# Attention on one core: the maxima's transposition, the one-over-sums products and VectorE's order rearranged

## The chip, the cores and the metric

The kernel runs on one core of one Trainium2 chip. The metric is the device time of one execution in microseconds; of several executions the median counts. A profiled execution has a time of its own and a span (first to last instruction), on which the trace is laid out.

## The reference, cut to what matters

One layer of a bidirectional encoder: attention, a residual layer norm, then a mixture of 32 experts (top 4 of 32, 1024 tokens) and another layer norm. The change touches attention alone. With 1024 tokens, 16 query heads in 4 groups of 4, and 64 values per head, the reference computes

```
q = rope(rms_norm(q)); k = rope(rms_norm(k))
for each block of 128 queries:
    s = einsum('bqkgd,bskd->bkgqs', q_blk, k) * HEAD_DIM ** -0.5
    p = softmax(s, axis=-1)
    o = einsum('bkgqs,bskd->bqkgd', p, v)
return o @ w_o
```

## The kernel before, in words

Attention runs as 32 groups: group n is a block of 128 queries (i = n // 4) with one group of four heads (g = n % 4). I call the groups of a block g0 to g3. Every group has eight steps k, one for each 128 keys. The loop over n and k near the end of the attention part writes out TensorE's order by hand (`manual_schedule` for PE); the orders of the other engines come from a planner, which may bring an instruction forward or put it off.

A step of group n issues on TensorE:

- `probs(n, k)`: two products into a PSUM tile `st` (128 keys by 512 queries; two such tiles in turn). The first is keys times queries, the second carries a correction and subtracts the maxima, which stand in rows 64 to 67 of the operand `q2s[n % 3]`. ScalarE then takes the exponential (`pt`), and GpSimd adds the eight `pt` of a group up in `acc`.
- `scores(n + 2, k // 2, k % 2)`: half of the scores of one head, two groups ahead, into a PSUM tile `sc` (two banks; two such tiles in turn). After the second half (odd k) VectorE takes the negated maximum over 1024 keys (line 434, tile `nm`). So each group has four of these maxima, m = 0 to 3, at k = 1, 3, 5 and 7.

Once in a group come:

- `maxima_a(n + 1)`: a transposition of the four maxima on TensorE (`tpm`, line 147) and on VectorE a product that spreads them over the rows of `q2s` (line 148). Its PSUM tile is one of tag `tp`, of which there is one buffer.
- `maxima_b(n + 1)`: ScalarE copies the queries into the other rows of `q2s`.
- `stack_q` (in g1 and g2): four transpositions (`tpq`, line 163) of the next block's queries, also into tag `tp`, which ScalarE (lines 165, 166) and VectorE (lines 167, 168) read.
- `pv(n - 1)`: 32 products of probabilities and values into the PSUM tile `po` (one buffer), and `close_a`, ScalarE's copy out of it.
- `late_sum(n - 1)`: VectorE adds the last `pt` to `acc` (line 452).

Once in a block of four groups come `scale_a` (in g0, behind `pv`: products `su` that sum over the keys, into tag `tp`, then on VectorE the reciprocal and three more instructions, lines 479 to 484) and `scale_b` (twice: a product `rb` into tag `tp` that spreads the reciprocals, and VectorE's product with the output, line 492).

Products and transpositions through the helper `mm` all show line 55. Each of the PSUM tags `tp` and `po` has one buffer, so a new tile of such a tag waits for all readers of the last one.

Of the kernel before, what the change touches and what calls it, by code (L numbers as in the profile page):

```python
# [9 lines left out]
F32 = mybir.dt.float32  # L10
# [10 lines left out]
P = 128  # L21
T = 1024
D = 1024
NT = T // P
# [3 lines left out]
HD = 64  # L28
# [17 lines left out]
def trunk_kernel(ctx: ExitStack, tc: tile.TileContext, x, w_qkv, q_norm, k_norm, w_o,  # L46
                 lnm_g, lnm_b, lnf_g, lnf_b, r_w, r_b, w_gu, b_gu, w_dn, b_dn,
                 rope_c, rope_s, out):
    nc = tc.nc
# [4 lines left out]
    def mm(o, lhsT, rhs, start=True, stop=True):  # L54
        nc.tensor.matmul(o, lhsT=lhsT, rhs=rhs, start=start, stop=stop)  # L55
# [49 lines left out]
    vn = p_kv.tile([P, NT, NKV, HD], F32, name="vn")  # L105
# [26 lines left out]
    def first_scores(s, ps):  # L132

        hf, m = divmod(s, 4)
        if s == 0:
            nms[0] = p_xq.tile([P, 4], F32R, tag="nm", bufs=3, name="nm0")
            nms["h"] = p_xq.tile([P, 4, 2], F32, name="nmh")
        sc = ps.tile([P, 512], F32, tag="qkv2", name=f"sc0_{s}")
        mm(sc, qs[0][:, m, :], kT_hi[:, 0, hf * 512:(hf + 1) * 512])
        nc.vector.tensor_reduce(nms["h"][:, m, hf:hf + 1], sc, AX.X, ALU.max, negate=True)  # L140
        if s == 7:
            nc.vector.tensor_reduce(nms[0], nms.pop("h"), AX.X, ALU.min)

    def maxima_a(n, ps):

        tp = ps.tile([P, 4, P], F32, tag="tp", name=f"tpm{n}")
        nc.tensor.transpose(tp[0:4, 0, :], nms.pop(n).bitcast(F32), ident)
        nc.vector.tensor_tensor(q2s[n % 3][HD:HD + 4], tp[0:4, 0:1, :].to_broadcast([4, 4, P]),  # L148
                                ident[0:4, 0:4, None].to_broadcast([4, 4, P]), ALU.mult)

    def maxima_b(n):
        i, g = divmod(n, NKV)
        nc.scalar.copy(q2s[n % 3][0:HD], qs[i][0:HD, 4 * g:4 * g + 4, :].bitcast(F32))
# [20 lines left out]
    with tc.tile_pool(name="p1", bufs=1, side="right", reuse_waits="tile") as p1, \  # L174
# [18 lines left out]
        def turn_x(i):  # L193
            xt = xts[i]
            xT = p_xq.tile([P, 2 * KD, P], F32R, tag="cols", bufs=2, name=f"xT{i}")
            hi, lo = xT[:, 0:KD, :], xT[:, KD:, :]
            for h in range(2):
                tp = ps1.tile([P, 4, P], F32, tag="tp", name=f"tp{i}_{h}")
                for c in range(4):
                    k = 4 * h + c  # L200
                    nc.tensor.transpose(tp[:, c, :], xt[:, k * P:(k + 1) * P], ident)
                split(hi[:, 4 * h:4 * h + 4, :], lo[:, 4 * h:4 * h + 4, :], tp)
            xTs[i] = (hi, lo)
            if i + 1 < NT:
                load_x(i + 1)
            else:
                load_q(0)

        def proj(i, k, j):
            hi, lo = xTs[i]  # L210
            sl = slice(j * 512, (j + 1) * 512)
            mm3(qkvs[i][j], hi[:, k, :], lo[:, k, :], wh[k][:, sl], wl[k][:, sl], k == 0, k == KD - 1)

        def open_qkv(i):
            t = {j: ps1.tile([P, 512], F32, tag=f"qkv{j}", name=f"qkv{i}_{j}") for j in (0, 2, 1)}
            qkvs[i] = [t[j] for j in range(3)]
# [4 lines left out]
        pe_order = ExitStack()  # L221
# [99 lines left out]
        for i in range(NT):  # L321
            k0 = (KD, late)[i] if i < 2 else 0
            if i > 1:
                open_qkv(i)
            for k in range(k0, KD):
                proj(i, k, 2)
            if 1 < i < NT - 1:
                turn_x(i + 1)
            norm_k(i)
            if i == NT - 1:  # L330
                stack_q(0, 0, ps1)
                stack_q(0, 1, ps1)
            for k in range(k0, KD):
                proj(i, k, 0)
                if i == NT - 1 and k % 2 == 1:
                    first_scores(k // 2, ps1)
            take_q(i, 0)
            if i == 0:
                take_q(i, 1)
            turn_k(i)  # L340
            if i == 0:
                turn_x(2)
            norm_q(i, 0)
            for k in range(k0, KD):
                proj(i, k, 1)
                if i == NT - 1 and 0 < k < 5:
                    first_scores(k + 3, ps1)
                if i == NT - 1 and k == 6:
                    maxima_a(0, ps1)
                    maxima_b(0)  # L350
            if i > 0:
                take_q(i, 1)
            norm_q(i, 1)
            if i == 1:
                in_order.close()
# [61 lines left out]
    with tc.tile_pool(name="p2", bufs=1, side="right", reuse_waits="tile") as p2, \  # L417
# [4 lines left out]
        pts, po, ot, sc, accs, rrs = [{} for _ in range(6)]  # L422
        NG = NT * NKV
# [27 lines left out]
        def late_sum(n):  # L451
            nc.vector.tensor_tensor(accs[n], accs[n], pts[n, NT - 1], ALU.add)

        def pv(n):

            i, g = divmod(n, NKV)
            po[n] = ps_o.tile([P, 2, P], F32, tag="po", name=f"po{n}")
            for k in range(NT):
                for a in range(2):
                    mm(po[n][a * HD:(a + 1) * HD].rearrange("p j t -> p (j t)"), vn[:, k, g, :],  # L460
                       pts[n, k][:, 2 * a * P:(2 * a + 2) * P], k == 0, k == NT - 1)
            for k in range(NT):
                del pts[n, k]

        def close_a(n):
            i, g = divmod(n, NKV)
            if g == 0:
                ot[i] = p2.tile([P, KD, P], F32, tag="ot", bufs=2, name=f"ot{i}")
            nc.scalar.copy(ot[i][:, 2 * g:2 * g + 2, :], po.pop(n))

        def scale_a(i):

            su = ps_t.tile([P, 4, P], F32, tag="tp", name=f"su{i}")
            for m in range(4):
                for g in range(NKV):
                    mm(su[g * NE:(g + 1) * NE, 0, :], which[:, m].rearrange("p r m -> p (r m)"),
                       accs[NKV * i + g][:, m * P:(m + 1) * P], m == 0, m == 3)
            rs = p2.tile([P, P], F32, tag="rs", bufs=1, name=f"rs{i}")
            nc.vector.reciprocal(rs, su[:, 0, :])
            hi = p2.tile([P, P], F32R, tag="rh", bufs=1, name=f"rh{i}")  # L480
            nc.vector.tensor_copy(hi, rs)
            nc.vector.scalar_tensor_tensor(rs, hi.bitcast(F32), low, rs, ALU.mult, ALU.subtract)
            rrs[i] = p2.tile([P, KD, P], F32R, tag="rr", bufs=1, name=f"rr{i}")
            nc.vector.tensor_tensor(rrs[i], rs[:, None, :].to_broadcast([P, KD, P]),
                                    col.rearrange("p g j -> p (g j)")[:, :, None].to_broadcast([P, KD, P]), ALU.mult)
# [39 lines left out]


        pe_order = ExitStack()
        pe_order.enter_context(tc.manual_schedule(engines={mybir.EngineType.PE}))
        for n in range(NG + 1):
            i, g = divmod(n, NKV)  # L530
            for k in range(NT):
                if k == (6 if n == 0 else 2) and n + 1 < NG:
                    maxima_a(n + 1, ps_t)
                if n < NG:
                    probs(n, k)
                if n == 0:
                    for m in range(2):
                        scores(1 + k // 4, k % 4, m)
                elif n + 2 < NG:
                    scores(n + 2, k // 2, k % 2)  # L540
                if n < NG and i + 1 < NT and g == 0 and k == 6:
                    load_q(i + 1)
                if k == (7 if n == 0 else 3) and n + 1 < NG:
                    maxima_b(n + 1)
                if k == 3 and n > 0:
                    if g in (1, 2) and i + 1 < NT:
                        stack_q(i + 1, g - 1, ps_t)
                    if n < NG - 1:
                        late_sum(n - 1)
                    pv(n - 1)  # L550
                    close_a(n - 1)
                    if g == 0:
                        scale_a(i - 1)
                if i > 0:
                    if (g, k) == (1, 5) or n == NG and k == 5:
                        scale_b(i - 1, 0)
                    if (g, k) == (1, 7) or n == NG and k == 7:
                        scale_b(i - 1, 1)
            if i in (2, 3) and g == 2:
                load_o(i - 2)  # L560
            if i == 4 and g == 2:
                load_xr(0)
# [790 lines left out]
    for i in range(NT // 2):  # L1353
        f = slot(order[(len(seq) + 1 + i) % len(order)], f"fs{i}")
# [13 lines left out]
    with tc.tile_pool(name="gen", bufs=1, side="right", reuse_waits="tile") as gp, \  # L1368
# [5 lines left out]
        with tc.For_i(0, n_blk, 1) as b:  # L1374
# [33 lines left out]
            for n in range(4):  # L1408
                w = gp.tile([P, KD, 512], F32, tag="gw", bufs=2, name=f"gwg{n}")
                nc.sync.dma_start(w, w_gu[ds(ev, 1), :, n * 512:(n + 1) * 512].rearrange("o (k p) n -> p (o k) n", p=P))  # L1410
                ps = gps.tile([P, 512], F32, tag="gu", bufs=2, name=f"ggu{n}")
# [6 lines left out]
            for n in range(2):  # L1418
                w = gp.tile([P, KD, 512], F32, tag="gw", bufs=2, name=f"gwd{n}")
                nc.sync.dma_start(w, w_dn[ds(ev, 1), :, n * 512:(n + 1) * 512].rearrange("o (k p) n -> p (o k) n", p=P))  # L1420
                ps = gps.tile([P, 512], F32, tag="gu", bufs=2, name=f"gy{n}")
# [87 lines left out]
```

## Time and profile before

| what | value |
|---|---|
| median of three runs | 2080.12 us (2079.3 to 2083.51) |
| the profiled execution's own time | 2075.34 us |
| its span | 2073.5 us |
| TensorE busy, of the span | 97% |
| VectorE, ScalarE, GpSimd busy, of the span | 77%, 62%, 26% |
| the 32 groups of attention | from 162 to about 520 us of the span |

TensorE's busy time counts the pipelined length of a product, which is longer than the spacing at which products follow one another. Where one engine's order is written by hand, its stalls are best read from the start times of neighbouring instructions: a step that has nothing to wait for shows the shortest spacing, and what goes beyond it is a wait or a switch.

### The profile page before, as it was taken

Reading aid. Unit: us, or ns where it says so; the run is one execution under the profiler, and the core shown is the slowest. Engines: PE = TensorE matmul, PEld = TensorE weight load, DVE = VectorE, ACT = ScalarE, POOL = GpSimd, SP = SyncE. Lnnn points to the kernel's source line nnn. Section 1 sums busy time; section 2 is a strip of 40 time slices with the busy share of each in tenths; the row PEclk is TensorE's granted clock in tenths of the full one; section 3 lists DMA queues with packets and bytes.
Section 4 is the critical chain, followed back from the end, with each engine's and each line's share of the span. In section 5 each row is a group of like instructions: output and inputs, shape, how many; then the busy total and the mean of one; then the engine's idle time right before and its main releaser. Section 6 shows DMA issues by size and latency. Waiting matters only on the chain. (4 is left out here: it accounts for less than half of the span.)

```text
span 2073.5 us, 28716 instructions
## 1 busy us (share of the span) xinstructions
PE 2011.8 (97%) x10691; PEld 1419.5 (68%) x10691; DVE 1601.8 (77%) x1649; ACT 1282.0 (62%) x1566; POOL 538.2 (26%) x373
## 2 busy tenths in 40 slices
PE   8998999999997999999999999999999999999997
PEld 6775666665675666666666767767777677677774
DVE  6647777776887877767777878878878788887894
ACT  5655655654554656566666766667667676676774
POOL 1216777775144211111102111101021121010100
PEclk9999999999998999999999999999999999999999
DMA  5216000000645777888788898978989889789875
GB/s 174 72 62 178 31 32 21 32 21 21 228 149 211 276 287 271 298 294 291 285 315 312 347 338 304 377 289 342 338 319 354 310 315 367 284 346 337 329 314 183
DMA packets 106352, 500.44 MB, mean 241 GB/s; under 512 B 16001, under 2 KB 17026, under 8 KB 73442
## 3 DMA queue, kind: packets, MB, share of 16 engines
q1 hardware_dynamic: 87360, 447.02, 56.0%
q0 software_dynamic: 16000, 50.90, 9.0%
q8 instruction: 85, 1.39, 0.3%
q10 hardware_dynamic: 2850, 0.66, 0.2%
q14 instruction: 57, 0.47, 0.1%
HBM read 457.05 MB, written 41.49 MB: 240 GB/s over the span
## 5 line engine op out<-in xcount | busy, mean ns | idle before, releaser
L55 PE MATMUL gu<-wh,xTh 128*128 128x512 f32 x1024 | 415.3, 406 | 1.0 <-ACT xTh L63 1.0
L55 PE MATMUL gu<-wh,xTl 128*128 128x512 f32 x1024 | 410.1, 400 | 0.0
L55 PE MATMUL gu<-wl,xTh 128*128 128x512 f32 x1024 | 401.9, 393 | 0.0
L1299 POOL DMA_INDIRECT fd<-y,mi x32 | 79.1, 2472 | 655.4 <-ACT y L1298 655.4
L448 POOL TENSOR_TENSOR acc<-acc,pt 128x512 f32<-128x512 f32 x152 | 211.8, 1394 | 78.3 <-ACT pt L444 68.7
L55 PEld LDWEIGHTS gu<-wh,xTh 128*128 128x128 f32 x1024 | 193.3, 189 | 42.4 <-ACT xTh L63 1.7
L55 PEld LDWEIGHTS gu<-wl,xTh 128*128 128x128 f32 x1024 | 193.3, 189 | 39.6 <-issue 0.2
L55 PEld LDWEIGHTS gu<-wh,xTl 128*128 128x128 f32 x1024 | 193.7, 189 | 38.8 <-issue 3.6
L55 PE MATMUL yp<-wl,aTh 128*128 128x512 f32 x512 | 204.2, 399 | 0.4 <-DVE wl L612 0.4
L55 PE MATMUL yp<-wh,aTh 128*128 128x512 f32 x512 | 201.6, 394 | 0.0
L55 PE MATMUL yp<-wh,aTl 128*128 128x512 f32 x512 | 199.7, 390 | 0.0
L434 DVE TENSOR_REDUCE nm<-sc 128x1 fp32r<-128x1024 f32 x124 | 150.6, 1221 | 50.5 <-PE sc L55 49.5
L444 ACT ACTIVATE pt<-st 128x512 f32<-128x512 f32 x256 | 149.4, 596 | 55.9 <-PE st L55 46.3
L598 POOL DMA_INDIRECT xg<-xd,mi x32 | 53.4, 1670 | 298.5 <-PE tpx L1136 288.9
L55 PE MATMUL qkv<-wh,xT 128*128 128x512 f32 x384 | 123.9, 403 | 2.6 <-ACT xT L63 1.4
L55 PEld LDWEIGHTS yp<-wh,aTh 128*128 128x128 f32 x512 | 96.2, 188 | 33.6 <-ACT act L1180 14.3
L55 PE MATMUL po<-pt,vn 128*64 128x256 f32 x1024 | 117.6, 382 | 0.0
L55 PE MATMUL st<-qs,kT_hi 128*128 128x512 f32 x256 | 112.5, 440 | 2.9 <-ACT pt L444 2.2
L55 PEld LDWEIGHTS yp<-wl,aTh 128*128 128x128 f32 x512 | 96.3, 188 | 21.9 <-DVE wl L612 1.2
L55 PEld LDWEIGHTS yp<-wh,aTl 128*128 128x128 f32 x512 | 96.1, 188 | 19.5
L55 PE MATMUL st<-q,kT_lo 128*128 128x512 f32 x256 | 102.2, 399 | 1.3 <-DVE q L148 1.3
L55 PE MATMUL sc<-kT_hi,qs 128*128 128x512 f32 x256 | 101.9, 404 | 1.0 <-DVE nm L434 0.8
(520 smaller groups left out, 4159.0 us busy)
## 6 DMA issues: line engine op xcount, KB each, us to landing
w0g<-in_expert_w_gate_up SPq DMA_DIRECT2D x8, 1024.0 KB, 7.1
w1g<-in_expert_w_gate_up SPq DMA_DIRECT2D x8, 1024.0 KB, 7.6
w2g<-in_expert_w_gate_up SPq DMA_DIRECT2D x8, 1024.0 KB, 9.6
w3g<-in_expert_w_gate_up SPq DMA_DIRECT2D x8, 1024.0 KB, 8.6
w4g<-in_expert_w_gate_up SPq DMA_DIRECT2D x8, 1024.0 KB, 6.9
w5g<-in_expert_w_gate_up SPq DMA_DIRECT2D x8, 1024.0 KB, 7.4
w6g<-in_expert_w_gate_up SPq DMA_DIRECT2D x8, 1024.0 KB, 6.5
w7g<-in_expert_w_gate_up SPq DMA_DIRECT2D x8, 1024.0 KB, 7.1
```

Of the source, the lines that this page charges most:

```text
L55: nc.tensor.matmul(o, lhsT=lhsT, rhs=rhs, start=start, stop=stop)
L434: nc.vector.tensor_reduce(nms[n][:, m:m + 1], sc.pop((n, m)), AX.X, ALU.max, negate=True)
L444: nc.scalar.activation(pts[n, k], st, AF.Exp)
L448: (nc.vector if n == NG - 1 or n == NG - 2 and k > 3 else nc.gpsimd).tensor_tensor(accs[n], pts[n, 0] if k == 1 else accs[n], pts[n, k], A ...
L598: return nc.gpsimd.indirect_dma_start(out=xg[e], out_offset=None, in_=xd, in_offset=bass.IndirectOffsetOnAxis(ap=mi[:, e:e + 1] if rows is ...
L1299: nc.gpsimd.indirect_dma_start(out=fd, out_offset=bass.IndirectOffsetOnAxis(ap=mi[:, e:e + 1], axis=0), in_=y, in_offset=None, bounds_chec ...
```

## The change

`maxima_a` takes its PSUM tile from its caller. For groups 2 to 31 the four maxima are transposed at step 3 instead of ahead of step 2, into columns 256 to 383 of the `po` tile, which is now a whole bank (512 columns), with the values' products behind it in columns 0 to 255. The call of `maxima_b` follows that of `stack_q`. `late_sum` keeps its place in g0 and moves to step 4, behind `pv`, in the other groups; the last `pt` of a group lives until then. The two `scale_b` move from g1 (steps 5 and 7) to g3 (steps 1 and 5). VectorE's order is written out too: inside the loop it follows the order of the code.

```
-    def maxima_a(n, ps):
+    def maxima_a(n, tp):
-        tp = ps.tile([P, 4, P], F32, tag="tp", name=f"tpm{n}")
         nc.tensor.transpose(tp[0:4, 0, :], nms.pop(n).bitcast(F32), ident)
...
-                    maxima_a(0, ps1)
+                    maxima_a(0, ps1.tile([P, 4, P], F32, tag="tp", name="tpm0"))
...
         def pv(n):
-            po[n] = ps_o.tile([P, 2, P], F32, tag="po", name=f"po{n}")
             for k in range(NT):
                 for a in range(2):
-                    mm(po[n][a * HD:(a + 1) * HD].rearrange("p j t -> p (j t)"), vn[:, k, g, :],
+                    mm(po[n][a * HD:(a + 1) * HD, 0:2, :].rearrange("p j t -> p (j t)"), vn[:, k, g, :],
                        pts[n, k][:, 2 * a * P:(2 * a + 2) * P], k == 0, k == NT - 1)
-            for k in range(NT):
+            for k in range(NT - 1):
                 del pts[n, k]
...
-            nc.scalar.copy(ot[i][:, 2 * g:2 * g + 2, :], po.pop(n))
+            nc.scalar.copy(ot[i][:, 2 * g:2 * g + 2, :], po.pop(n)[:, 0:2, :])
...
-        pe_order.enter_context(tc.manual_schedule(engines={mybir.EngineType.PE}))
+        pe_order.enter_context(tc.manual_schedule(engines={mybir.EngineType.PE, mybir.EngineType.DVE}))
         for n in range(NG + 1):
             i, g = divmod(n, NKV)
             for k in range(NT):
-                if k == (6 if n == 0 else 2) and n + 1 < NG:
-                    maxima_a(n + 1, ps_t)
+                if n == 0 and k == 6:
+                    maxima_a(n + 1, ps_t.tile([P, 4, P], F32, tag="tp", name="tpm1"))
                 if n < NG:
                     probs(n, k)
...
-                if k == (7 if n == 0 else 3) and n + 1 < NG:
+                if n == 0 and k == 7:
                     maxima_b(n + 1)
                 if k == 3 and n > 0:
+                    po[n - 1] = ps_o.tile([P, 4, P], F32, tag="po", name=f"po{n - 1}")
+                    if n + 1 < NG:
+                        maxima_a(n + 1, po[n - 1][:, 2:3, :])
                     if g in (1, 2) and i + 1 < NT:
                         stack_q(i + 1, g - 1, ps_t)
-                    if n < NG - 1:
+                    if n + 1 < NG:
+                        maxima_b(n + 1)
+                    if g == 0 and n < NG - 1:
                         late_sum(n - 1)
                     pv(n - 1)
                     close_a(n - 1)
                     if g == 0:
                         scale_a(i - 1)
+                if k == 4 and g > 0 and 0 < n < NG - 1:
+                    late_sum(n - 1)
                 if i > 0:
-                    if (g, k) == (1, 5) or n == NG and k == 5:
+                    if (g, k) == (3, 1) or n == NG and k == 5:
                         scale_b(i - 1, 0)
-                    if (g, k) == (1, 7) or n == NG and k == 7:
+                    if (g, k) == (3, 5) or n == NG and k == 7:
                         scale_b(i - 1, 1)
```

## Rows read from the trace of the kernel before

**Rows 1.** Windows view: two stretches, busy times of each engine, granted clock, DMA.

```profile
187.40:200.90 13.50, 10.62 (x63) 6.83 (x62) 8.62 (x8) 7.35 (x14) 7.99 (x7) 1.00 1.04 232
...
342.93:386.92 43.99, 42.23 (x271) 27.53 (x271) 34.05 (x34) 25.77 (x46) 33.03 (x25) 1.00 0.07 25
```

**Rows 2.** Waits view, 162 to 520 us: total us, times, longest.

```profile
PE tpq L163 <- DVE q L148: 7.4, 14, 2.8
...
PE tpm L147 <- DVE nm L434: 3.9, 7, 0.6
```

**Rows 3.** Timeline, TensorE, end of a g2 and start of the g3 behind it.

```profile
376.67 0.40 PE L55 MATMUL sc<-kT_hi,qs 128*128 128x512 f32 x1
376.91 0.47 PE L55 MATMUL st<-qs,kT_hi 128*128 128x512 f32 x1
...
378.16 0.40 PE L55 MATMUL sc<-kT_hi,qs 128*128 128x512 f32 x1
...
378.72 0.50 PE L55 MATMUL st<-qs,kT_hi 128*128 128x512 f32 x1
...
379.99 0.40 PE L55 MATMUL sc<-kT_hi,qs 128*128 128x512 f32 x1
380.32 3.67 PE L55 MATMUL po<-pt,vn 128*64 128x256 f32 x32
```

**Rows 4.** Timeline, TensorE, the g1 and g2 ahead of it.

```profile
354.35 0.40 PE L55 MATMUL sc<-kT_hi,qs 128*128 128x512 f32 x1
...
355.06 0.40 PE L55 MATMUL sc<-kT_hi,qs 128*128 128x512 f32 x1
...
356.10 0.48 PE L55 MATMUL st<-qs,kT_hi 128*128 128x512 f32 x1
...
357.35 0.40 PE L55 MATMUL sc<-kT_hi,qs 128*128 128x512 f32 x1
357.92 0.66 PE L163 MATMUL tpq<-ident,ql 128*128 128x128 f32 x4 [0.17 <-DVE q L148]
358.50 3.67 PE L55 MATMUL po<-pt,vn 128*64 128x256 f32 x32
...
365.01 0.40 PE L55 MATMUL sc<-kT_hi,qs 128*128 128x512 f32 x1
...
366.14 0.40 PE L55 MATMUL st<-qs,kT_hi 128*128 128x512 f32 x1
...
368.81 0.40 PE L55 MATMUL sc<-kT_hi,qs 128*128 128x512 f32 x1
...
370.31 3.67 PE L55 MATMUL po<-pt,vn 128*64 128x256 f32 x32
```

**Rows 5.** Timeline, VectorE, the same block.

```profile
350.96 0.96 DVE L479 RECIPROCAL rs<-su 128x128 f32<-128x128 f32 x1 [0.53 <-PE su L55]
...
354.80 2.35 DVE L434 TENSOR_REDUCE nm<-sc 128x1 fp32r<-128x1024 f32 x2
357.18 0.68 DVE L148 TENSOR_TENSOR q<-tpm,ident 4x512 fp32r<-4x512 f32 x1
...
365.06 0.69 DVE L492 TENSOR_TENSOR ot<-ot,rb 128x512 f32<-128x512 f32 x1
...
377.11 1.22 DVE L434 TENSOR_REDUCE nm<-sc 128x1 fp32r<-128x1024 f32 x1 [0.27 <-PE sc L55]
```

**Rows 6.** Timeline, VectorE, the last `scale_a`, with nothing between its instructions.

```profile
519.91 0.96 DVE L479 RECIPROCAL rs<-su 128x128 f32<-128x128 f32 x1 [2.88 <-PE su L55]
...
521.55 1.22 DVE L484 TENSOR_TENSOR rr<-rs,col 128x1024 fp32r<-128x1024 f32 x1
```

**Rows 7.** Timeline, ScalarE and VectorE, the readers of `tpq` in group 2.

```profile
194.36 0.58 ACT L165 CAST qs<-tpq 64x512 fp32r<-64x512 f32 x1 [3.11 <-PE tpq L163]
194.96 0.58 ACT L166 CAST odd<-tpq 64x512 fp32r<-64x512 f32 x1
...
195.57 0.68 DVE L167 TENSOR_TENSOR qs<-tpq,qs 64x512 fp32r<-64x512 f32 x1 [0.71 <-ACT odd L166]
```

## Prediction

> **What bounds the kernel now.** I read the windows view first, cut at the first product of each group, to see what a steady block of four groups costs: 43.99 us, with TensorE busy for 42.23 of them and the clock granted in full [rows 1]. VectorE has 34 us of work in it and ScalarE 26, so TensorE is the bound, and what counts is what makes TensorE wait or switch. The waits view of the attention stage comes next. TensorE's waits there are few: 7.4 us for line 148 ahead of the transpositions of `stack_q`, 3.9 us of the maxima's transposition for the last maximum [rows 2]. They are what this change can win. The TensorE timeline then gives prices by neighbouring starts. The reader is to see three spacings in it. A product follows `sc` after 0.24 us when nothing intervenes; with the maxima's transposition between, the spacing is 0.56 us, so it costs 0.32 [rows 3]. In g1 the same place takes 1.04 us, so 0.80 more than normal, since the transposition there waits for a maximum [rows 4]. And from the `sc` of step 3 to the first product of `pv` it takes 0.33 us in g3 (and, as the steps repeat, in g0), 1.15 in g1 and 1.50 in g2, where `stack_q` and its wait lie between [rows 3, 4].
>
> **What the move to the values' bank does.** The transposition itself moves to where TensorE changes over to `pv` anyway, and its 0.32 us (0.80 in g1, next to nothing in g2) leave step 1. But VectorE's line 148 now reads the bank into which `pv` writes next, and `pv` stands behind it in the code. The question is whether `pv` has to wait for that read although the columns differ. The trace has a case of its own: line 167 reads partitions 0 to 63 of a `tpq` tile and needs, as data, only line 165. Line 165 ended at 194.94, VectorE was idle, and yet line 167 began at 195.57, 0.03 us after the end of line 166, which reads partitions 64 to 127 of the same tile [rows 7]. So in this program accesses by two engines to one PSUM bank wait for each other, even reads of different halves. I take it that `pv` waits for line 148.
>
> The Trainium skill, "PSUM — Partial Sum Buffer", section "PSUM bank collisions raise a hardware error", states that two engines must not be at one bank in the same 32 partitions at one time, whichever addresses they touch. Line 148 reads partitions 0 to 3 and `pv` begins in partitions 0 to 63, so by that rule the wait is needed and the sum is the one below; a guard by address would give rival A's time. The trace is stricter than the rule, which lets different quadrants of a bank go together, as lines 166 and 167 would be.
>
> **The price of that wait.** In the code order that VectorE now follows, the maximum m = 1 of step 3 stands ahead of line 148, since `scores` is called before `maxima_a`. From the start of the last `sc` product: 0.44 us until VectorE begins the maximum (376.67 to 377.11) [rows 3, 5], 1.23 for it, 0.03 to the next instruction (354.80 + 2.35 to 357.18), 0.68 for line 148 [rows 5], 0.06 until TensorE goes on (357.86 to 357.92) [rows 4, 5]. `pv` starts 2.44 us behind `sc`, where it started after 0.33, 1.15 or 1.50. The step so gains 2.11 us in g0 and g3, 1.29 in g1, 0.94 in g2. The transpositions of `stack_q` (0.58 us, [rows 4]) no longer wait for line 148, and lie inside the wait. The transposition's own wait for the maxima ends too: they are ready over a step earlier. Nothing else hides these 2.44 us: the exponentials ahead are done and those behind need `st` products that stand behind `pv`.
>
> **The one-over-sums products.** In g1 they cost two spacings and a wait: step 5 one product (0.24), step 7 from `sc` to `st` 1.13 instead of 0.24, so 0.89 [rows 4], together 1.13. In g3 I charge one spacing each, 0.48. There is a side effect in g3: VectorE's product for the first of them (0.69, [rows 5]) now stands ahead of the step-3 maximum. It ends 0.44 + 1.23 + 0.03 + 0.69 = 2.39 us after the `sc` of step 1 and VectorE is ready 0.03 later; the `sc` of step 3 comes 1.83 - 0.32 = 1.51 behind that of step 1 [rows 3], plus the `rb` product 0.24, and is complete 0.44 later, at 2.19. The maximum, and so `pv`, are 0.23 late. The store of the block's output on SP's queue comes half a block later; it is read a block after that at the earliest, and I cost it at nothing.
>
> **VectorE's written order.** In g0 the planner slipped a maximum in ahead of the last instruction of `scale_a`. In code order the four instructions run through: 519.91 to 522.77, 2.86 us [rows 6]. From 350.96 that ends at 353.82, the maximum m = 2 follows until 355.08, and with 0.06 for the signal the `sc` of the next g1, which needs its buffer, can start at 355.14 instead of 354.35 [rows 4, 5]: 0.79 us. It can be as little as nothing, should the planner's order be kept. `late_sum` costs nothing on TensorE: in g0 it has all of `pv` (3.6 us) before `su` needs it, in the others it runs under `pv`; VectorE has some 10 idle us in a block [rows 1]. What it stops doing is to delay maxima, and that gain is in the removed waits already.
>
> **The sum.** Of a block, in us: g0 2.11 - 0.32 = +1.79. g1 +1.29 - 0.80 - 1.13 + 0.79 = +0.15. g2 +0.94. g3 +2.11 + 0.23 - 0.32 + 0.48 = +2.50. Together +5.38, and for blocks 1 to 6, six times, +32.3. The ends by the same terms: group 1 as g1 without the other terms +1.29; group 2 +0.94 less the 2.3 us by which its wait of 2.8 exceeds that of a usual g2 (0.5), -1.36 [rows 2]; group 3 +1.79; group 28 as g0 +1.79; group 29 +2.11 - 0.80 - 1.13 + 0.79 = +0.97; group 30, which has no maximum ahead of line 148, about +0.7 (the wait 1.0, the transposition -0.3); group 31 takes the two `rb`, +0.48. That is +5.7. In all +38 us, so the profiled execution would go from 2075.34 to 2113. The median before is 4.8 above that execution, which I carry over: 2080.1 + 38 = 2118 us.
>
> The bounds of this case: without the 0.79, seven times, and the terms of groups 30 and 31, it is +31; with 0.2 us more at each of thirty waits, as a switch of TensorE to other work costs in these rows (0.09 to 0.32), +44. With the spread of the runs before this case alone spans 2108 to 2128.
>
> **Rivals.** A, faster: `pv` doesn't wait, because columns are told apart. Then step 3 costs 0.1 more in g0 and g3 and loses the `stack_q` wait, 0.3 in g1 and 0.6 in g2. A block has -0.2, -1.45, -0.6, +0.3, so -2.0, six of them -12, and the ends -4 (group 2's long wait above all): 2064 us. For it speaks that the columns do differ; against it that lines 166 and 167 are disjoint too and still wait [rows 7]. It decides as soon as `pv` starts less than 1.15 us behind `sc` on the mean: that is the 0.83 of before (the mean of 0.33, 1.15, 1.50 and 0.33) and a quarter of the 1.30 that a block's other terms take away. Chance 0.11.
>
> B, no change to speak of: `pv` waits, but line 148 comes ahead of the maximum on VectorE, because VectorE's order is not that of the code after all. Then it starts when the transposition is through, 0.24 + 0.35 behind `sc`, and `pv` after 0.24 + 0.35 + 0.68 + 0.06 = 1.33, 1.11 less than above. Thirty times that takes 33 of the 38 us away, and g3's 0.23 go as well: 2083 us. For it speaks that the planner did put other work between; against it that TensorE's order, written in the same way, is that of the code in every row I read. Chance 0.05.
>
> A clock that falls because TensorE now rests would be worse than all of these. In group 2 TensorE sat for 2.8 us already and the clock stayed at its upper level in that stretch (1.00, TensorE busy for 10.62 of 13.50 us) [rows 1, 2]; a block after the change would be busier. I leave it outside.
>
> **How the numbers follow.** The first case has 0.84, and its sum is the prediction. A run of this kernel can tell some 0.2% from no change, 4 us. All of the first case is slower, all of A faster, B about the same: 0.84, 0.11, 0.05. The range 2096 to 2132 leaves A and B out, 0.16, and holds the first case with its bounds and something for terms I can't see, below it in particular, where the removed waits may be worth more.
>
> **What the profile after would show.** TensorE waits `po <- q` some 30 times, about 1.5 to 2 us each, and `tpq <- q` gone. If A is right there is no such wait. The step from the last `sc` to `po` is 2.4 us in g0 and 2.7 in g3; if it is 1.3, B. A block takes 49.4 us. `sc <- nm` appears at the start of g1 with 0.8. `rb` stands alone in g3 with no wait. The prediction is wrong if the two accesses to the bank overlap, or if the maximum of step 3 is not ahead of line 148.

## The result, and the profile after

The changed kernel takes 2139.18 us (median of 4 runs, 2136.28 to 2141.45) against 2079.71 before: a ratio of 1.0294, 95% interval 1.028 to 1.0308. It is slower, by 59 us where I forecast 38, and outside my range. The profiled execution took 2136.28 us with a span of 2134.5, 61.0 us more than the span before.

The waits view of the attention stage, kernel after (total us, times, longest). In the changed file lines 146, 147, 152, 162, 433, 443, 447, 451, 482 and 490 are the former 147, 148, 153, 163, 434, 444, 448, 452, 484 and 492, and the maxima's transposition shows the name `po`.

```profile
PE po L55 <- DVE q L147: 50.4, 30, 1.9
...
PE sc L55 <- DVE nm L433: 11.0, 8, 1.5
```

The thirty forecast waits of `pv` for the product on VectorE are there, 50.4 us in all, and the 7.4 us of `tpq <- q` and the 3.9 of the maxima's transposition [rows 2] are gone. The second row is a wait that I had put at 0.8 us each time; the longest is 1.5.

The timeline of group 12 (a g0) after, from the last `sc` of step 3 on, TensorE and VectorE:

```profile
318.79 0.40 PE L55 MATMUL sc<-kT_hi,qs 128*128 128x512 f32 x1
...
319.02 0.27 PE L146 MATMUL po<-ident,nm 128*4 128x128 f32 x1
319.23 1.23 DVE L433 TENSOR_REDUCE nm<-sc 128x1 fp32r<-128x1024 f32 x1 [0.47 <-PE sc L55]
...
320.48 0.68 DVE L147 TENSOR_TENSOR q<-po,ident 4x512 fp32r<-4x512 f32 x1
...
321.22 3.67 PE L55 MATMUL po<-pt,vn 128*64 128x256 f32 x32 [1.92 <-DVE q L147]
```

From `sc` to the first product of the values it is 321.22 - 318.79 = 2.43 us; 2.44 was the forecast, against 0.33 before [rows 3]. The maximum, line 147 and the signal follow one another as summed up.

The same place in group 16, also a g0, after:

```profile
369.62 0.40 PE L55 MATMUL sc<-kT_hi,qs 128*128 128x512 f32 x1
...
372.04 5.36 PE L55 MATMUL po<-pt,vn 128*64 128x256 f32 x32 [1.92 <-DVE q L147]
```

The wait is the same, but the 32 products behind it take 5.36 us instead of 3.67. The windows view tells why. These are four stretches of the kernel after: a block without and a block with such lengthened products, then the products of groups 16 and 12 alone. The eighth column is the granted clock.

```profile
315.85:366.68 50.83, 42.34 (x272) 27.72 (x271) 33.19 (x35) 25.66 (x46) 32.14 (x26) 1.00 0.09 32
366.68:420.87 54.19, 45.72 (x272) 29.30 (x271) 34.13 (x35) 25.66 (x46) 31.47 (x25) 0.94 0.06 20
...
372.04:377.33 5.29, 5.29 (x32) 2.97 (x32) 1.58 (x1) 0.00 (x0) 1.03 (x1) 0.68 0.02 3
321.22:324.82 3.60, 3.60 (x32) 2.21 (x32) 0.67 (x1) 0.00 (x0) 1.75 (x1) 1.00 0.16 63
```

Behind the wait of group 16 the clock was at its lower level for most of `pv` (0.68 granted over all of it), in group 12 it was not (1.00). A block has 50.83 us without such a stretch, against 43.99 [rows 1] and the 49.4 that I forecast; the next block has two stretches and 54.19, so each costs 1.7 us. Six groups of this execution have one, all g0 or g3, where TensorE waits longest.

### The profile page after: what moved, and what is told of

Read it like the earlier page. It is cut to its first block, busy times and chain, and to the rows that moved or that the text cites. A ratio compares the mean times of both kernels' runs of the same rounds, so it can differ in the third digit from the quotient of the medians.

```text
span 2134.5 us, 28711 instructions
## 1 busy us (share of the span) xinstructions
PE 2025.5 (95%) x10691; PEld 1425.7 (67%) x10691; DVE 1600.6 (75%) x1649; ACT 1281.4 (60%) x1566; POOL 532.1 (25%) x373
## 5 line engine op out<-in xcount | busy, mean ns | idle before, releaser
L447 POOL TENSOR_TENSOR acc<-acc,pt 128x512 f32<-128x512 f32 x152 | 201.0, 1322 | 146.5 <-ACT pt L443 136.8
L55 PEld LDWEIGHTS gu<-wl,xTh 128*128 128x128 f32 x1024 | 193.2, 189 | 39.5 <-issue 0.2
L55 PE MATMUL po<-pt,vn 128*64 128x256 f32 x1024 | 127.7, 406 | 50.4 <-DVE q L147 50.4
L55 PEld LDWEIGHTS po<-pt,vn 128*64 128x64 f32 x1024 | 75.4, 145 | 98.9 <-DVE q L147 60.4
```

Source lines behind the costliest of these rows:

```text
L447: (nc.vector if n == NG - 1 or n == NG - 2 and k > 3 else nc.gpsimd).tensor_tensor(accs[n], pts[n, 0] if k == 1 else accs[n], pts[n, k], A ...
```

## The experiments

Times are medians; each kernel's ratio is against runs of the kernel before taken along with it (2077 to 2078 us). Edits are given against the changed kernel.

**Maxima back in a tile of tag `tp`** (`e1_tp`)

```
-                        maxima_a(n + 1, po[n - 1][:, 2:3, :])
+                        maxima_a(n + 1, ps_t.tile([P, 4, P], F32, tag="tp", name=f"tpm{n + 1}"))
```

> The changed kernel, except that the maxima are transposed into a tile of tag tp again (still at step 3). Theory W, that the products of the values wait for VectorE's line 148 because both touch one bank, and that this is most of the loss: in g0 and g3 the first product comes 0.3 us after the last sc instead of 2.4, and in g1 and g2, where the transpositions of stack_q now stand between, 0.58 later than in the changed kernel. With 15 groups at -2.1, group 30 at -1.0 and 14 groups at +0.58 that is -24 us; the six half-clock stretches of 3.4 us, all behind the long waits of g0 and g3, should go too, -10 us. Time 2105 us. Rival O, that VectorE's written order and the moved products cost the time and the wait only shows where TensorE would stand anyway: 2139 us, within 5.

2114.23 us, ratio 1.018 (1.0163 to 1.0197), so 25 us less than the changed kernel, and 9 more than expected. The waits view, this run:

```profile
PE tpq L162 <- DVE q L147: 26.9, 14, 1.9
```

No row `po <- q` is left. The wait has moved to the transpositions of `stack_q` in g1 and g2, 14 times 1.9 us. The 24 us of theory W came, the 10 us of the clock did not: the granted clock from 200 to 540 us is 0.97, as after the change, and the lower level now sits behind the 1.9 us waits of g1 and g2. Rival O falls: same written order, same moved products, 25 us less.

**Maxima a step earlier, still in the values' bank** (`e2_early`)

```
+                if k == 2 and n > 0:
+                    po[n - 1] = ps_o.tile([P, 4, P], F32, tag="po", name=f"po{n - 1}")
+                    if n + 1 < NG:
+                        maxima_a(n + 1, po[n - 1][:, 2:3, :])
                 if k == 3 and n > 0:
-                    po[n - 1] = ps_o.tile([P, 4, P], F32, tag="po", name=f"po{n - 1}")
-                    if n + 1 < NG:
-                        maxima_a(n + 1, po[n - 1][:, 2:3, :])
```

> The changed kernel, except that po is opened and the maxima are transposed into it behind the scores of step 2, so that line 148 comes ahead of the maximum m = 1 on VectorE. Theory W: line 148 then ends some 2.4 us after the sc of step 1, the first product of the values would be due 1.9 us after it; the wait shrinks from 1.9 us to 0.5 in g0, to nothing in g1 and g2, and to about 1.2 in g3, where line 490 stands ahead. That is -41 us over 30 groups, and no half-clock stretch, -10: 2088 us. Rival A', that a wait of this kind is there whatever the distance, since a bank that TensorE has written is held until the whole of VectorE's queue has passed: 2139 us.

2079.75 us, ratio 1.0009 (1.0 to 1.0019): nearly all of the loss is gone, and the time is 8 us below theory W's. The waits view, this run:

```profile
PE sc L55 <- DVE nm L433: 11.1, 8, 1.5
PE po L55 <- DVE q L147: 6.3, 15, 0.7
```

The wait for line 147 has shrunk from 50.4 to 6.3 us, at most 0.7 at a time, and the granted clock from 200 to 540 us is 1.00 again. The values' products still write behind a reader of their bank; but the transposition comes a step earlier, so line 147 stands ahead of the maximum m = 1 in VectorE's order and TensorE has the products of step 3 to do meanwhile. The edit changes both at once, and what each is worth by itself is not shown. Rival A' falls. The wait of `sc` stays at 11 us and is the next to look at.

**VectorE's order left to the planner** (`e3_planner`)

```
-        pe_order.enter_context(tc.manual_schedule(engines={mybir.EngineType.PE, mybir.EngineType.DVE}))
+        pe_order.enter_context(tc.manual_schedule(engines={mybir.EngineType.PE}))
```

> The changed kernel, except that VectorE's order is left to the planner again. In that order the late sum stands ahead of the maximum m = 0 or m = 1 in three groups of four, and the maximum m = 2 of g0 stands ahead of the last instruction of scale_a. Theory W: what is ahead of line 148 on VectorE is what the values wait for, so the late sum, with its wait for GpSimd, adds about 1.3 us to the wait in three groups of four, 22 times, +29 us, and the 1.75 us at step 0 of g1 go, 7 times, -12 us: about 2156 us. Rival O, that the written order costs the time: 2127 us or less.

2184.55 us, ratio 1.0512 (1.0494 to 1.0529). Rival O falls again, and theory W named the direction but not the size, 29 us too little. The waits view and the timeline of VectorE in a g3, this run:

```profile
PE po L55 <- DVE q L147: 89.9, 30, 4.5
```

```profile
268.77 1.75 DVE L451 TENSOR_TENSOR acc<-acc,pt 128x512 f32<-128x512 f32 x1 [1.23 <-POOL acc L447]
270.45 1.21 DVE L433 TENSOR_REDUCE nm<-sc 128x1 fp32r<-128x1024 f32 x1
271.58 0.67 DVE L490 TENSOR_TENSOR ot<-ot,rb 128x512 f32<-128x512 f32 x1
272.18 1.21 DVE L433 TENSOR_REDUCE nm<-sc 128x1 fp32r<-128x1024 f32 x1
273.42 0.68 DVE L147 TENSOR_TENSOR q<-po,ident 4x512 fp32r<-4x512 f32 x1
```

The late sum waits 1.23 us for GpSimd and stands ahead of two maxima and line 490; line 147 comes behind them all, and the wait of `pv` grows to as much as 4.5 us. The thirty waits are 39.5 us longer than in the changed kernel, where theory W had 29, and the granted clock from 200 to 540 us is 0.93 instead of 0.97, which theory W left out. With `pv` tied to line 147, the written order is what keeps the damage small.

**TensorE kept at work in the wait** (`e7_fill`); the seven extra products are in g0 and g3 and nobody reads them

```
+                    if g in (0, 3) and n + 1 < NG:
+                        fill = ps_t.tile([P, 4, P], F32, tag="tp", name=f"fill{n}")
+                        for _ in range(7):
+                            mm(fill.rearrange("p j t -> p (j t)"), kT_hi[:, 0, 0:P], kT_hi[:, 0, 0:512])
```

> The changed kernel with seven extra products of 512 columns in every g0 and g3, behind the maxima's transposition, into a tile of tag tp that nobody reads. They take 1.65 us of the 1.9 us in which TensorE waits for line 148 and change no result. Theory C, that the six stretches at half clock come from TensorE resting there: none is left between 200 and 500 us, -10 us, 2129 us. Rival: the stretches come by themselves, whatever TensorE does: as many as before, 2139 us or some us more.

2126.9 us, ratio 1.0238 (1.0221 to 1.0256): 12 us less with more work. Windows view, 200 to 540 us, first the changed kernel, then this one:

```profile
200.00:540.00 340.00, 285.03 (x1766) 184.24 (x1765) 219.30 (x220) 164.63 (x296) 204.16 (x157) 0.97 0.08 29
```

```profile
200.00:540.00 340.00, 305.54 (x1901) 201.05 (x1901) 228.72 (x226) 169.09 (x303) 212.76 (x162) 1.00 0.08 29
```

The clock is full throughout, and no `pv` is lengthened. Theory C stands: the lower level came from TensorE resting in g0 and g3.

**The last instruction of `scale_a` later** (`e5_rr_late`): line 482 becomes a function `scale_c` of its own

```
+                if k == 4 and (g == 1 and i > 0 or n == NG):
+                    scale_c(i - 1)
```

> The changed kernel, except that the last instruction of scale_a (VectorE's line 482 of the changed kernel, 2.2 us where GpSimd adds at the same time) is issued at step 4 of g1, while TensorE is in the values' products, instead of in g0 ahead of the maximum m = 2. Theory P, that the scores at step 0 of g1 wait for this maximum behind a lengthened line 482: step 0 of g1 goes from 2.5 us to 0.8, 7 times, and line 482 takes 1.2 us where GpSimd rests. -12 us, 2127 us, give or take the number of half-clock stretches. Rival: the wait is that of a buffer that ScalarE or TensorE frees, and stays: 2139 us.

2124.85 us, ratio 1.0221 (1.0206 to 1.0237), 14 us less. The view of the tile `rr`, its writer on VectorE (count, shortest/median/longest ns), first the changed kernel, then this one, and the latter's wait of `sc`:

```profile
L482 DVE TENSOR_TENSOR rr<-rs,col x8: 1225/2202/2206, 225.9 to 579.9; 128x1024 fp32r<-128x1024 f32 x8
```

```profile
L486 DVE TENSOR_TENSOR rr<-rs,col x8: 1210/1218/1225, 234.1 to 572.1; 128x1024 fp32r<-128x1024 f32 x8
```

```profile
PE sc L55 <- DVE nm L433: 0.8, 1, 0.8
```

The instruction (line 486 in this run's file) is back at 1.22 us and the wait at step 0 of g1 is gone. As it no longer stands ahead of the maximum, the whole wait went, not only what the lengthening added. What lengthened it shows in the timeline of the changed kernel, group 12 and the first step of the g1 behind it:

```profile
327.40 3.52 POOL L447 TENSOR_TENSOR acc<-acc,pt 128x512 f32<-128x512 f32 x2 [4.39 <-ACT pt L443]
...
327.61 2.20 DVE L482 TENSOR_TENSOR rr<-rs,col 128x1024 fp32r<-128x1024 f32 x1
...
329.73 2.34 DVE L433 TENSOR_REDUCE nm<-sc 128x1 fp32r<-128x1024 f32 x2
...
331.00 0.19 PEld L55 LDWEIGHTS sc<-kT_hi,qs 128*128 128x128 f32 x1 [1.91 <-DVE nm L433]
```

It begins 0.21 us into the first of two additions on GpSimd, which takes 1.32 us, and lasts 0.98 us longer than by itself, about the rest of that addition. The maximum m = 2 starts behind it, and the `sc` of g1 waits for that. By the Trainium skill, "SBUF — State Buffer", section "Who interferes with whom", a VectorE instruction with two SBUF inputs and a GpSimd instruction that reads SBUF exclude one another, and the one issued first holds the port to its end. The trace agrees: 2.20 us behind the addition's start, 1.22 with GpSimd at rest.

**ScalarE's order written too** (`e6_act`)

```
-        pe_order.enter_context(tc.manual_schedule(engines={mybir.EngineType.PE, mybir.EngineType.DVE}))
+        pe_order.enter_context(tc.manual_schedule(engines={mybir.EngineType.PE, mybir.EngineType.DVE, mybir.EngineType.Activation}))
```

> The changed kernel with ScalarE's order written out as well, so that the copy of the queries for the next group comes at step 3, where TensorE waits, instead of at step 0 or 1, where the planner puts it. Theory S, that the long step 1 (1.03 us in g2, 0.88 in g0) comes from this copy on ScalarE and never came from the maxima's transposition: step 1 is 0.70 to 0.80 in g0 and g2, and about 0.95 in g3, which has a product more. -0.6 us a block, 4 us in all: 2135 us. Rival: step 1 keeps its length, since it belongs to TensorE's switch between kinds of products: 2139 us.

2131.64 us, ratio 1.0266 (1.0249 to 1.0283), 7.5 us less. The stretches at the lower clock differ from run to run; free of them is the length of a g2 whose products are not lengthened, 12.10 us after the change and 11.75 here. The timeline of the g2 of the changed kernel, start of the group:

```profile
342.96 0.62 ACT L152 CAST q<-qs 64x512 fp32r<-64x512 f32 x1
...
343.49 1.07 ACT L443 ACTIVATE pt<-st 128x512 f32<-128x512 f32 x2
343.56 0.40 PE L55 MATMUL sc<-kT_hi,qs 128*128 128x512 f32 x1
344.13 0.19 PEld L55 LDWEIGHTS st<-qs,kT_hi 128*128 128x128 f32 x1 [0.61 <-ACT pt L443]
344.13 0.50 PE L55 MATMUL st<-qs,kT_hi 128*128 128x512 f32 x1 [0.17 <-ACT pt L443]
```

The spacing from `sc` to `st` at step 1 is 0.57 us, the same 0.56 that I had read as the price of the transposition [rows 3]. No transposition stands there any more: the copy of the queries holds the exponentials up, and `st` waits for them. The kernel before has the copy ahead of the same exponentials in its g3, where the `st` of 378.72 [rows 3] comes behind the first of them:

```profile
377.56 0.62 ACT L153 CAST q<-qs 64x512 fp32r<-64x512 f32 x1
378.08 1.07 ACT L444 ACTIVATE pt<-st 128x512 f32<-128x512 f32 x2
```

With the copy at step 3 the 0.33 us are gone, as the same place of the g2 of this run shows. Theory S stands.

```profile
344.61 0.39 PE L55 MATMUL sc<-kT_hi,qs 128*128 128x512 f32 x1
...
344.83 0.47 PE L55 MATMUL st<-qs,kT_hi 128*128 128x512 f32 x1
```

**The products `rb` back in g1** (`e4_scale_g1`)

```
-                    if (g, k) == (3, 1) or n == NG and k == 5:
+                    if (g, k) == (1, 5) or n == NG and k == 5:
-                    if (g, k) == (3, 5) or n == NG and k == 7:
+                    if (g, k) == (1, 7) or n == NG and k == 7:
```

> The changed kernel with the two products rb back at steps 5 and 7 of g1. If their move was a gain, as the prediction has it (1.13 us a block in g1 against some 0.2 to 0.5 in g3), the time rises by 0.6 to 0.9 us in each of 7 blocks, to 2144 us. If the move is part of the loss, because line 490 stands ahead of the maxima in g3, it falls below 2136.

2149.3 us, ratio 1.0321 (1.0275 to 1.0367), from 2133.6 to 2151.32. The granted clock from 200 to 540 us is 0.94 in its profile (0.97 after the change): thirteen groups have lengthened products there, six after the change, and seven more at 1.7 us are 12 us. So the size of the move's own gain can't be read from the medians. It can be read from blocks with the same number of lengthened groups: with two, from the values' products of one g0 to those of the next, it is 54.53 us here (326.89 to 381.42) and 54.20 after the change (372.04 to 426.24). The move gained 0.33 us a block, where 0.6 to 0.9 was expected; it was no part of the loss.

**Three costs off at once** (`e8_three`): the edits of `e7_fill`, `e5_rr_late` and `e6_act`

> The changed kernel with three of the suspected costs taken away at once: the extra products that keep TensorE at work in the wait of g0 and g3, the last instruction of scale_a at step 4 of g1, and ScalarE's order written out. If these three are all that the prediction missed, what is left is the wait for line 148 as predicted: in g0 12.6 us, in g1 11.6, in g2 11.75, in g3 12.15, together 48.1 a block, 4.1 more than before; about 2139 - 12 - 12 - 4 = 2111 us, and the single gains add up. If they overlap (a stall that only moves to the next wait), 2118 us or more.

2111.36 us, ratio 1.0157 (1.0137 to 1.0177). Windows view of one block, this run:

```profile
308.91:357.28 48.37, 44.91 (x285) 30.05 (x285) 32.41 (x35) 26.42 (x46) 31.16 (x26) 1.00 0.10 34
```

48.37 us, 48.1 expected: in a block the three add up, and what is left of the loss, 4.4 us, agrees with the forecast wait for line 147 less the waits that the change took away. The median is 28 us below the changed kernel's, as expected, while the three single falls measured 12, 14 and 7.5; the difference of 6 us stays open.

**A version that beats both** (`b1_early_rr`, `b2_early_rr_act`): the maxima a step earlier as in `e2_early`, `scale_c` as in `e5_rr_late`, the first `rb` at step 5 of g2; the second version with ScalarE's order written as well

```
-                    if (g, k) == (3, 1) or n == NG and k == 5:
+                    if (g, k) == (2, 5) or n == NG and k == 5:
```

> Three things together: the maxima transposed behind the scores of step 2 as in the run with that alone (2079.75 us), the last instruction of scale_a at step 4 of g1, and the first of the two products rb at step 5 of g2 instead of step 1 of g3, so that line 490 doesn't stand ahead of line 148 there. If what is left of the loss is the wait at step 0 of g1 (1.74 us, 7 times) and the wait in g3 (0.4 us more than in g0, 7 times): 2079.8 - 12.2 - 2.8 = 2065 us, 0.6% faster than before. If the block is held by something else (ScalarE's chain): 2075 us or more.

> The run before this one with ScalarE's order written out too. If step 1 is long for the copy of the queries, another 4 us: 2061 us. If not, 2065 us, or more where a copy in written order holds an exponential up.

2066.15 us, ratio 0.9948 (0.9933 to 0.9963), and 2061.58 us, ratio 0.992 (0.9907 to 0.9934). Windows view of one block, the second version:

```profile
291.60:334.00 42.40, 41.51 (x272) 27.61 (x271) 32.02 (x35) 26.46 (x46) 31.55 (x26) 1.00 0.11 38
```

42.40 us against 43.99 before [rows 1], with TensorE busy for all but 0.9 of them.

## Why the prediction was right or wrong

**Right: `pv` waits for line 148 although the columns differ.** Thirty waits, 50.4 us, and none of them left where the maxima go into a tile of tag `tp` instead (`e1_tp`). Rival A is out, and so is B, since the maximum stands ahead of the line in the order as written and the step measured 2.43 us for 2.44. `e2_early` gave nearly all of it back with the line ahead of the maximum and a step earlier. No run separates the bank from the tile: `po` is one tile and one bank, and so is `tpq` in rows 7.

**Wrong: "A clock that falls because TensorE now rests would be worse than all of these ... I leave it outside."** This is the step that failed most. I argued from one wait of 2.8 us in group 2 behind which the clock stayed up. One wait without a fall doesn't show that the next thirty have none: six of thirty had one here, 1.7 us each, 10.2 us. The sum had nothing for it, since I thought of it as a case of its own, worse than all others, where it came in short pieces. `e7_fill` showed the cause: 12 us less, clock 1.00.

**Mis-sized: "0.79 us" for the maximum behind the written-out `scale_a`.** Step 0 of g1, from its first product to that of step 1, has 2.51 us (328.82 to 331.33) for 0.77 before (353.82 to 354.59), 1.74 more. I took 2.86 us for the four instructions from the last `scale_a`, where GpSimd rests [rows 6]; in a block GpSimd adds, and the last instruction takes 2.20 instead of 1.22. The 0.95 us that the term lacks are 6.7 us in seven blocks. `e5_rr_late` gave 14 us back with 12 expected, the whole wait.

**Wrong: "so it costs 0.32" for the transposition, taken out of g0 and g3.** The spacing was ScalarE's, held up by its copy of the queries. In g3 it is 0.56 after the change too (355.67 to 356.23), with the first `rb` inside it; in g0 it was never 0.56 but 0.42 (344.18 to 344.60) and is 0.42 after (317.10 to 317.52); and it appears in g2, where the planner now puts the copy there too. `e6_act` removes it.

**Not there: the 0.23 us by which line 490 was to delay the maximum in g3.** From the last `sc` to `pv` it is 2.43 us in g3 too (357.52 to 359.95). The term rested on the same 0.32: as step 1 keeps its length, the `sc` of step 3 comes 1.85 us behind that of step 1 (355.67 to 357.52), not 1.75, and the maximum and line 490 occupy VectorE until 2.25 us behind the latter (357.92), not 2.39. With the copy moved away (`e6_act`), 0.10 of it is seen: 2.53 us (409.82 to 412.35). So the products' move was worth 0.33 us a block (`e4_scale_g1`), where my terms make it 0.42 (1.13 less 0.48 and 0.23).

The sum in rows: a block without a clock stretch is 50.83 us, 6.84 more than before, where I had 5.38; six blocks are 41 us for 32. By groups it is 2.08, 1.18, 1.33 and 2.25 us in g0 to g3, where I had 1.79, 0.15, 0.94 and 2.50: the missing gain of 0.32 in g0, the copy in g2, the longer `scale_a` in g1, and in g3 the 0.23 that did not come. The six stretches add 10.2. The remaining 10 us, for which I had 5.7, lie at the two ends of the stage, some 7, and behind it: TensorE's last `rb` comes 58.4 us later than before (582.81 for 524.46), the end 61.0. Where the 2.6 us behind the stage come from was not sought.

## What to carry to other kernels

Before two results share a PSUM bank to free another, look at who reads the first and what stands ahead of that reader in its engine's queue: in this program the next writer of the bank waited for all of it, though it wrote other columns. If the sharing must be, put the reader early and ahead of long work in its queue; here one step earlier turned 1.0294 into 1.0009.

A spacing between two instructions is not the price of what stands between them until the same place without it has been seen. And a duration taken from a quiet place (the last group) can be too short for a busy one: 1.22 us against 2.20 here.

## What the runs showed of the hardware that I had not expected

A wait of 1.9 us on TensorE was followed by its lower clock level in some cases and not in others, among waits alike to 0.01 us (1.92 in groups 12 and 16): in six of thirty groups of the changed kernel's profile, in thirteen of that of `e4_scale_g1`. Each fall cost 1.7 us in the products behind it. Products that nobody reads, issued in the wait, kept the clock up and made the kernel 12 us faster (2139.18 to 2126.9). What decides which of the waits is followed by a fall I did not settle.

VectorE's line 482 takes 1.22 us alone and 2.20 us when it begins 0.21 us into a GpSimd addition. Before the change the same instruction ran in 1.22 us in the midst of the same additions: with the planner's order it began (353.67) as the first of them ended, and the second, begun at 353.80, took 2.22 us where an addition by itself takes 1.27. There GpSimd, which is off TensorE's path, bore the collision. So a reordering of VectorE can change an instruction's length by 80% without touching it.
